# Attention's value projection computed as seven half-size products with the tokens stationary, its weight sums made in memory, and the input operands loaded ahead of it

## The chip, the cores and the metric

The kernel runs on one core of one Trainium2 chip. The metric is the device time of one execution in microseconds (us), as the median of several runs. Five engines run their own instruction streams and wait for each other by semaphores: PE (matrix multiplication, with its weight loads shown as PEld), DVE (vector), ACT (scalar, activations), POOL (GpSimd) and SP, which in this kernel only issues DMA transfers. Line numbers such as L256 are those of the kernel before.

## The reference, cut to what matters

One encoder layer over 512 tokens of width 2048, in float32:

```python
h = rms_norm(x, norm_mix_w[i])
proj = h @ w_in[i]
q_a, k_a, v_a, q_g, k_g, v_g, r_g, gate_lr = split_cols(proj, IN_SPLITS)
y_a = chunked_band_attention(q_a, k_a, v_a, att_rel_bias[i])     # 16 heads of 64
...
o_g = gated_linear_attention(q_g, k_g, v_g, log_a)               # 4 heads, state recurrence
o_g = rms_norm(o_g, gla_norm_w[i])
y_g = o_g * jax.nn.silu(r_g)
x = x + jnp.concatenate([y_a, y_g], axis=-1) @ w_out[i]
...                                                              # conv MLP, embedding, norm
```

The change concerns `v_a = h @ w_in[:, 2048:3072]` alone: 512 tokens by 2048 by 1024 columns.

## The kernel before, in words

**Number format.** Every float32 product is made of three matmuls on two-part operands. A weight page (128 x 1024, 512 KB) is loaded raw; ACT writes its high half (rounded), DVE its low half (raw less high); then high x high, high x low and low x high are accumulated. `wtile` (L118) does this for the first stages: it takes the next of three raw pages, three high pages and three low pages in rotation (the rings of L32), issues the load from SP, and queues the two halves on ACT and DVE. So the split of page n waits until PE is done with page n-3, and the load of page n+3 waits for the split of page n. It also pops one entry of the list `chores` (L116), if there is one.

**Stages.** First comes the normalised input `h1` (16 tiles of 128 x 2 x 512). Then, all from `h1`: the values of the linear attention (two calls of `vproj`, L234), then for its four heads a key and a query projection (`gla_proj`, L1150; `pk`, `pq`, 48 matmuls of 512 columns each) and the recurrence (`gla_core`, L1198: transposes `pkt`, scores `pat`, state updates `pu`, outputs `po`, a norm that goes through the sums `msw` and the root `rg`). Attention's values (`values_a`, L1076) are two more calls of `vproj`: the 128-token slices of `h1` are stationary, 512 weight columns move, 192 matmuls each, on 16 weight pages. `values_a(0)` stands before the last recurrence, `values_a(1)` after it.

After them the rest of the layer runs as Strassen-Winograd products: a 2 x 2 block product by seven half-size products P1, P2, P6, P5, P7, P3, P4 (L29) with the input operands R11, R21, N2, N1, T3, R22, T4 and the weight blocks or sums L11, L12, S2, S1, S3, S4, L22. The seven operands of the stage "in" (`front`) are made from the input early, by `input_pair`, and stored in memory as `h1d`; `Stage.load` (L342) brings each back in two tiles g = 0, 1 (512 KB each), and `Stage.split` (L348) makes its halves on ACT and DVE. Before the change six of these tiles (R11, R21, N2) are loaded after the linear attention's buffers are gone and split inside `values_a(1)` (`operand_step`); the other eight are loaded after it, when `h1` is free (`operands_left`), N1 is split there and T3, R22, T4 in the first steps of the stage.

**Sums in memory.** For some units the weight sums S1 to S4 are made by DMA: `sum_begin` copies one block to a scratch page in memory, and `sum_add`, issued by POOL, accumulates the other onto it. `chores` holds 18 such steps, for the first units of "wo" and "up", popped one at each `wtile` of the four heads.

**Order.** The Tile layer places the instructions of the early stages itself. Where the wrappers `vec`, `act`, `ten` (L55) are switched on, instructions stay in the order in which they are written; before the change that holds from the step loop on. On each engine the built order is fixed, and an instruction that waits holds up all behind it. The step loop takes a list `agenda` by step number.

Of the kernel before, what the change touches and what calls it, by code (L numbers as in the profile page):

```python
# [8 lines left out]
F32 = mybir.dt.float32  # L9
# [21 lines left out]
            "PP": ("L11", None, None)}  # L31
PLAIN = ("P1", "P2", "P6", "P5", "P7", "P3", "P4")  # L32
# [9 lines left out]
def encoder_block(ctx: ExitStack, tc: tile.TileContext, A, out):  # L42
# [27 lines left out]
    vec, act, ten = InOrder(nc.vector), InOrder(nc.scalar), InOrder(nc.tensor)  # L70

# [44 lines left out]
    chores = []  # L116

    def wtile(src, name, parts=1, between=None):  # L118
# [4 lines left out]
        for i in range(parts):  # L123
            if i and between is not None:
                between()
            c = slice(i * w, (i + 1) * w)
            nc.sync.dma_start(raw[:, c], src[:, c])
            nc.scalar.activation(hi[:, c], raw[:, c], AF.Copy)
            nc.vector.tensor_tensor(lo[:, c], raw[:, c], hi[:, c].bitcast(F32), ALU.subtract)
        if chores:  # L130
            chores.pop(0)()
# [102 lines left out]
    def vproj(src, c, evict, first=False, between=None, then=None):  # L234
        ps = [psum_mm(f"v{c}_{t}") for t in range(TT)]
        for kp in range(KD // 2):
            xs = []
# [65 lines left out]
    X_TAGS = [(op, g) for op in ("R11", "R21", "N2", "N1", "T3", "R22", "T4") for g in range(2)]  # L303

    def xtile(op, g, name, dt=F32R):
        pool = xa[0] if X_TAGS.index((op, g)) < 6 else xb[0]
        return pool.tile([P, 2, 1024], dt, tag=f"{op}{g}", name=name)
# [647 lines left out]

    for i, f in enumerate(sum_chores(summed[4:])):
        agenda[base[stages[4].units[2]] + 5 * i].append((0, f))
# [116 lines left out]
    vstage = {}  # L1074

    def values_a(c, between=None, then=None):  # L1076
        def place(t):
            vstage[c, t] = xslot(4 * c + t, "va")
            return vstage[c, t]

        vproj(A["w_v_a"], c, place, between=between, then=then)
        for t in range(TT):
            (nc.scalar if c else nc.sync).dma_start(vad[4 * c:4 * c + 4, :, t].rearrange("b p v -> p b v"),
                              vstage[c, t].rearrange("p (b v) -> p b v", b=4))
# [3 lines left out]
    with ExitStack() as mix:  # L1088
        vp = mix.enter_context(tc.tile_pool(name="v", bufs=1, side="right"))

        with ExitStack() as gctx:
# [21 lines left out]
            for c in range(2):  # L1113
                vproj(A["w_v_g"], c, lambda t: V[:, t, c * T:(c + 1) * T], c == 0, input_pair if c else None)

# [34 lines left out]
            def gla_proj(hd):  # L1150
# [39 lines left out]
                nc.vector.tensor_tensor(dd, kf, dd, ALU.mult)  # L1190
                pq = psum_mm("pq")
                proj(pq, [A["w_blk"][16 + hd, i] for i in range(2)], h1, f"wqg{hd}")
                qf = gt("qf", "kf")
                nc.vector.scalar_tensor_tensor(qf, pq, float(P) ** -0.5, rb, ALU.mult, ALU.mult)
                nc.vector.tensor_tensor(eb, qf, eb, ALU.mult)
                return eb, en, dd, dec2

            def gla_core(hd, eb, en, dd, dec2):  # L1198
# [3 lines left out]
                nc.vector.tensor_tensor(by_chunk(kd2), by_chunk(dd), each(dec2[:, 0:NCH]), ALU.mult)  # L1202
                eb2 = gt("eb2", "eb2")
                nc.vector.tensor_tensor(by_chunk(eb2), by_chunk(eb), each(dec2[:, NCH:2 * NCH]), ALU.mult)
                pkt = psum_aux("pkt")
                for t in range(TT):
                    sl = slice(t * P, (t + 1) * P)
                    nc.tensor.transpose(pkt[:, sl], kd2[:, sl], ident)
                kT = gt("kT", "kT")
                nc.scalar.activation(kT, pkt, AF.Copy)  # L1210
                pat = psum_aux("pat")
                for t in range(TT):
                    sl = slice(t * P, (t + 1) * P)
                    nc.tensor.matmul(pat[:, sl], en[:, sl], eb[:, sl], start=True, stop=True)
                for t in range(TT):
                    e0, o0 = t * P, t * P + CHUNK
                    nc.tensor.matmul(pat[0:CHUNK, o0:o0 + CHUNK], dd[:, e0:e0 + CHUNK], eb[:, o0:o0 + CHUNK],
                                     start=True, stop=True)
                at = attn_t[hd % 2]
                nc.vector.copy_predicated(at.rearrange("p (t j) -> p t j", j=P),  # L1220
                                          causal[:, None, :].broadcast_to([P, TT, P]),
                                          pat.rearrange("p (t j) -> p t j", j=P))

                S = [None] * TT
                for t in range(TT - 1):
                    pu = psum_aux("pu")[:, 0:256]
                    nc.tensor.matmul(pu, kT[:, t * P:(t + 1) * P], V[:, t, hd * 256:(hd + 1) * 256], start=True, stop=True)
                    S[t + 1] = gt(f"S{t + 1}", f"S{t + 1}", 1, 256)
                    if t == 0:
                        nc.vector.tensor_copy(S[1], pu)  # L1230
                    else:
                        d = 2 * NCH + t
                        nc.vector.scalar_tensor_tensor(S[t + 1], S[t], dec2[:, d:d + 1], pu, ALU.mult, ALU.add)

                o = []
                s2 = gt("s2", "s2")
                for vb in range(2):
                    po = psum_aux("po")
                    for t in range(TT):
                        sl = slice(t * P, (t + 1) * P)  # L1240
                        c0 = hd * 256 + vb * P
                        nc.tensor.matmul(po[:, sl], V[:, t, c0:c0 + P], at[:, sl], start=True, stop=t == 0)
                        if t > 0:
                            nc.tensor.matmul(po[:, sl], S[t][:, vb * P:(vb + 1) * P], eb2[:, sl], start=False, stop=True)
                    ov = xslot(8 + 2 * hd + vb, f"o{hd}_{vb}")
                    nc.vector.tensor_copy(ov, po)
                    if vb == 0:
                        nc.scalar.activation(s2, ov, AF.Square)
                    else:
                        s3 = tp.tile([P, T], F32, tag="sq", name="s3")  # L1250
                        nc.scalar.activation(s3, ov, AF.Square)
                        nc.vector.tensor_tensor(s2, s2, s3, ALU.add)
# [3 lines left out]
                nc.scalar.activation(sh, s2, AF.Copy)  # L1256
                nc.vector.tensor_tensor(sl, s2, sh.bitcast(F32), ALU.subtract)
                rstd_wide(ones_r, (sh, sl), 256, rg, gt("nwa", "nwa"))
                for vb in range(2):
                    nc.vector.scalar_tensor_tensor(o[vb], o[vb], gnw[:, vb:vb + 1], rg, ALU.mult, ALU.mult)  # L1260
# [321 lines left out]
```

## Time and profile before

| | |
|---|---|
| three runs | 2261.85, 2261.94, 2263.08 us; median 2261.94 |
| span of the profiled execution, first to last instruction | 2260.4 us |
| PE busy | 2245.6 us (99%), 18008 matmuls |
| DVE busy | 1859.7 us (82%) |
| ACT busy | 1298.9 us (57%) |
| DMA moved | 565.02 MB, 250 GB/s in the mean |

The page gives the span of the profiled execution; its own device time is not printed beside it, so 2260.4 is compared with the runs, which lie 1.5 us above it. "Busy" is the sum of the shown durations. A matmul's duration runs from its start to its modelled end and overlaps the next one, so the rate is read from the starts. A row of the timeline has the start and duration in us, the engine, the line, the operation, output<-inputs, shape, how many are merged, and in brackets how long the engine was idle before it and who ended that. Rows with SPq are DMA issues, not transfers.

### The profile page before, as it was taken

To read this page: it belongs to the slowest core of one execution; us is meant where nothing else is said; L and a number is where in the kernel's file an instruction comes from. 1 tells how busy PE (TensorE), PEld (TensorE's weight loads), DVE (VectorE), ACT (ScalarE), POOL (GpSimd) and SP (SyncE) were. 2 spreads that over 40 slices of the span, in tenths; PEclk is the share of its full clock that TensorE was granted. 3 is DMA by queue.
4 is the path that set the end of the run, shared out by engine and by line. 5 is a ranking of instruction groups with operands and counts; after the bars stand their busy time and mean duration, and the time that the engine had idled before them with its cause. 6 is when DMAs were issued, how large, how long until landed. Compare 5 with 4: busy or idle time off the path is not lost.

```text
span 2260.4 us, 45099 instructions
## 1 busy us (share of the span) xinstructions
PE 2245.6 (99%) x18008; PEld 2178.9 (96%) x18008; DVE 1859.7 (82%) x2562; ACT 1298.9 (57%) x1913; POOL 169.7 (8%) x209
## 2 busy tenths in 40 slices
PE   9999999999999999999999999999999999999997
PEld 8888889999999999999999999999999999999997
DVE  7567368998788888999888888888898797898987
ACT  6354367776665665555555555555564554666765
POOL 0010000000000001111111110000000100000000
PEclk9999999999999999999999999999999999999998
DMA  6994496666988979999999987877866967879896
GB/s 217 286 251 140 168 302 171 181 185 183 334 295 252 329 238 261 296 283 291 282 269 288 264 231 209 218 215 200 247 244 228 302 222 225 327 247 331 285 292 207
DMA packets 208882, 565.02 MB, mean 250 GB/s; under 512 B 22464, under 2 KB 73920, under 8 KB 208672
## 3 DMA queue, kind: packets, MB, share of 16 engines
q1 hardware_dynamic: 177536, 459.60, 57.3%
q0 software_dynamic: 27648, 99.10, 24.0%
q10 hardware_dynamic: 3488, 3.44, 0.4%
q8 instruction: 141, 2.31, 0.4%
q14 instruction: 69, 0.57, 0.1%
HBM read 483.41 MB, written 124.78 MB: 269 GB/s over the span
## 4 chain that ended last, share of the span: by engine, by line
PE 93%; DVE 3%; DMA 1%; ACT 1%; issue 1%; DVEq 0%; SPq 0%; POOL 0%; ACTq 0%; POOLq 0%
PE accA L64 44%; PE accC L64 22%; PE accB L64 11%; PE v L256 3%; PE v L258 3%; PE v L257 3%; PE pp L64 1%; PE psc L64 1%; PE ptr L64 1%; PE py L64 1%; DMA on<-ond 1%; DVE wl L64 1%; PE pq L137 1%; PE pq L136 0%; PE pq L135 0%
## 5 line engine op out<-in xcount | busy, mean ns | idle before, releaser
L64 DVE TENSOR_TENSOR wl<-s,wh 128x1024 fp32r<-128x1024 f32 (+1 forms) x365 | 438.1, 1201 | 67.2 <-ACT wh L64 66.3
L64 ACT ACTIVATE wh<-l 128x1024 fp32r<-128x1024 f32 (+1 forms) x308 | 319.0, 1037 | 184.4 <-PE accC L64 116.8
L64 DVE TENSOR_TENSOR wl<-l,wh 128x1024 fp32r<-128x1024 f32 (+1 forms) x308 | 367.8, 1194 | 57.4 <-ACT wh L64 57.1
L64 ACT ACTIVATE wh<-s 128x1024 fp32r<-128x1024 f32 (+1 forms) x365 | 378.1, 1036 | 28.2 <-DVE s L64 15.5
L64 ACT ACTIVATE u<-accA 128x256 f32<-128x256 f32 x290 | 109.6, 378 | 364.8 <-PE accA L64 364.7
L64 DVE TENSOR_TENSOR s<-s,l 128x1024 f32<-128x1024 f32 (+1 forms) x168 | 201.5, 1200 | 5.6 <-DMA s<-in_w_blk 5.2
L64 PE MATMUL accA<-up_T,wh 128*128 128x256 f32 x1408 | 178.8, 279 | 0.0
L64 PEld LDWEIGHTS accA<-up_T,wh 128*128 128x128 f32 x1408 | 170.3, 188 | 0.0
L64 DVE SCALAR_TENSOR_TENSOR cv<-u,cw,cv 128x511 f32<-128x511 f32 (+1 forms) x176 | 131.6, 748 | 3.1
L419 POOL DMA_DIRECT2D s<-in_w_up x84 | 74.2, 883 | 737.1 <-DMA s<-in_w_up 332.4
L256 PE MATMUL v<-wv_h,h 128*128 128x512 f32 x256 | 100.3, 392 | 0.0
L258 PE MATMUL v<-wv_h,h 128*128 128x512 f32 x256 | 100.1, 391 | 0.0
L257 PE MATMUL v<-wv_l,h 128*128 128x512 f32 x256 | 99.6, 389 | 0.0
L64 PE MATMUL accA<-up_T,wl 128*128 128x256 f32 x704 | 96.6, 279 | 0.0
L64 PE MATMUL accA<-dn_T,wh 128*128 128x256 f32 x704 | 89.9, 279 | 0.0
L64 PE MATMUL accA<-up_R,wh 128*128 128x256 f32 x704 | 89.8, 280 | 0.0
L64 PE MATMUL accB<-up_R,wh 128*128 128x256 f32 x704 | 89.4, 279 | 0.0
L64 PE MATMUL accC<-up_N,wh 128*128 128x256 f32 x704 | 89.4, 279 | 0.0
L64 PE MATMUL accC<-up_R,wh 128*128 128x256 f32 x704 | 89.4, 279 | 0.0
L64 PE MATMUL accA<-up_N,wh 128*128 128x256 f32 x704 | 89.4, 279 | 0.0
L64 PEld LDWEIGHTS accA<-up_T,wl 128*128 128x128 f32 x704 | 88.1, 188 | 0.0
L64 DVE TENSOR_TENSOR u<-u,accC 128x256 f32<-128x256 f32 x98 | 41.0, 418 | 57.2 <-PE accC L64 56.1
(410 smaller groups left out, 5131.6 us busy)
## 6 DMA issues: line engine op xcount, KB each, us to landing
l<-in_w_up SPq DMA_DIRECT2D x132, 512.0 KB, 6.5
s<-in_w_up SPq DMA_DIRECT2D x84, 512.0 KB, 6.0
s<-in_w_up POOLq DMA_DIRECT2D x84, 512.0 KB, 7.2
l<-in_w_dn SPq DMA_DIRECT2D x56, 448.0 KB, 5.0
l<-in_w_blk SPq DMA_DIRECT2D x36, 512.0 KB, 4.8
l<-in_w_out SPq DMA_DIRECT2D x28, 512.0 KB, 5.0
l<-in_w_dn SPq DMA_DIRECT2D x28, 512.0 KB, 4.9
s<-in_w_blk SPq DMA_DIRECT2D x24, 512.0 KB, 4.7
```

What stands on the lines that cost most here:

```text
L64: ins = f(*args, **kw)
L137: nc.tensor.matmul(po, wlo, act[:, 0, :], start=False, stop=stop)
L256: nc.tensor.matmul(ps[t], h1[kt][:, 0, sl], wh, start=kt == 0, stop=False)
L257: nc.tensor.matmul(ps[t], h1[kt][:, 0, sl], wl, start=False, stop=False)
L258: nc.tensor.matmul(ps[t], h1[kt][:, 1, sl], wh, start=False, stop=kt == KD - 1)
L419: nc.gpsimd.dma_start(t, src("L22" if name == "S1" else "L11"), accum_op=ALU.add)
```

## The change

**The product.** `values_a` goes. Attention's values become seven products of half size, from the operand tiles of `front` instead of `h1`: per product 4 weight pages, per page two blocks of 128 rows, two token slices, three matmuls of 512 columns, so 12 matmuls per page, 28 pages, 336 matmuls in all against 384. Four pages of each of P1, P2, P4 come from the weights; P6, P5, P7, P3 read pages S2, S1, S3, S4 that 16 DMA copies and 16 accumulating DMAs have made in memory (18 `value_chores`, four of them popped in the first `vproj`, the others in the four heads, none in the second `vproj`). The seven results are gathered by ACT and DVE into four quarters and stored to `vad`.

```diff
+    def values_begin():
+        v = dict(ps=[psum_mm(f"va{i}") for i in range(4)], pages=[(p, j) for p in PLAIN for j in range(4)], tiles={}, have=set())
+        for n in range(2):
+            value_fetch(v, n)
+        return v
+    def value_fetch(v, n):
+        if n < len(v["pages"]):
+            prod, j = v["pages"][n]
+            v["tiles"][n] = wtile(value_page(PRODUCTS[prod][0], j), f"wva_{prod}{j}")
+    def values_product(v, prod, between=None):
+        _, op, b = PRODUCTS[prod]
+        acc2 = v["ps"][0:2] if b == "A" else v["ps"][2:4]
+        fresh = prod in ("P1", "P2", "P5")
+        for j in range(4):
+            n = 4 * PLAIN.index(prod) + j
+            value_fetch(v, n + 2)
+            if between is not None:
+                between(j)
+            hi, lo = v["tiles"].pop(n)
+            for i in range(2):
+                k = 2 * j + i
+                x = front.x[op, k // 4]
+                wh, wl = hi[:, i * T:(i + 1) * T], lo[:, i * T:(i + 1) * T]
+                for t in range(2):
...
+                    ten.matmul(acc2[t], x[:, 0, sl], wh, start=first, stop=False, **kw)
+                    ten.matmul(acc2[t], x[:, 0, sl], wl, start=False, stop=False, **kw)
+                    ten.matmul(acc2[t], x[:, 1, sl], wh, start=False, stop=last, **kw)
+    def values_collect(v, prod):
...
+            if quarter not in v["have"]:
+                act.activation(dst, acc2[i], AF.Copy, scale=float(sign))
+            else:
+                vec.tensor_tensor(dst, dst, acc2[i], ALU.add if sign > 0 else ALU.subtract)
+            if quarter in v["have"] or quarter == "C21":
+                (nc.scalar if c else nc.sync).dma_start(vad[4 * c:4 * c + 4, :, 2 * h + i].rearrange("b p v -> p b v"),
...
```

**Its place.** It needs the operands, so `h1`'s buffers are given up and the first eight operand tiles (R11, R21, N2, N1) are loaded into them right after the last head's query projection; the other six follow after P2. What is left of the last two recurrences (`gla_core` is now a generator) is written between the pages of P1 and P2, with the wrappers on, so in written order. The splits of all operands stand between the pages, those of T3, R22, T4 no longer in the step loop.

```diff
-            for hd in range(1, 4):
+            for hd in range(1, 3):
                 nxt = gla_proj(hd)
-                gla_core(hd - 1, *st)
+                for _ in gla_core(hd - 1, *st):
+                    pass
                 st = nxt
-            values_a(0)
-            gla_core(3, *st)
+            cores = [gla_core(2, *st)]
...
+            nxt = gla_proj(3, middle)
+            cores.append(gla_core(3, *nxt))
+            hctx.close()
...
+            for op, g in X_TAGS[:8]:
+                front.load(op, g)
+            in_order(True)
+            va = values_begin()
+            for g in range(2):
+                front.split("R11", g)
+            step(0)
+            nxt[-1]()
+            def beside_first(j):
+                if j:
+                    step(0)
+                if j > 1:
+                    front.split("R21", j - 2)
+                    step(1)
+            def beside_second(j):
+                step(1)
+                if j % 2:
+                    front.split("N2", j // 2)
+            values_product(va, "P1", beside_first)
+            values_collect(va, "P1")
+            values_product(va, "P2", beside_second)
+            values_collect(va, "P2")
...
+    for op, g in X_TAGS[8:]:
         front.load(op, g)
...
+    values_product(va, "P6", lambda j: front.split("N1", j // 2) if j % 2 else None)
+    values_collect(va, "P6")
+    values_product(va, "P5", lambda j: front.split("T3", j // 2) if j % 2 else None)
...
```

**The other sums.** The 18 chores of "wo" and "up" move from the heads into the step loop:

```diff
+    for i, f in enumerate(sum_chores(summed[:4])):
+        agenda[2 + 5 * i + 3 * max(i - 10, 0)].append((0, f))
...
-    for n, op in enumerate(("T3", "R22", "T4")):
-        for g in range(2):
-            agenda[2 * n + g + (n > 0)].append((3, lambda op=op, g=g: front.split(op, g)))
...
-            chores.extend(sum_chores(summed[:4]))
```

**The built order around it** (P10 is page 0 of P1, and so on; "high" and "low" are the halves of a page or an operand tile; "a > b" means that b stands behind a):

```
PE    last pq: 20 matmuls > pkt, pat of head 2 > 28 matmuls > pu > P10 > po > P11 > msw > P12 >
      pkt, pat of head 3 > P13 > pu > P20 > po > P21 > msw > P22 > P23 > P60 ... P43 (12 matmuls each) > pp
ACT   high P10 > kT > high P11 > high R11.0 > high R11.1 > high P12 > high P13 > two squares > s2h >
      high P20 > Ln > Exp (rg) > high R21.0 > high P21 > high R21.1 > kT ...
      second norm: s2h > high N2.0 > high P60 > Ln > Exp > high P61
DVE   kf > low P10 > en, dd, kd2, eb2 > mask > low P11 > low R11.0 > low R11.1 > three states S > two for eb >
      low P12 > low P13 > two copies of po > sum > s2l > low P20 > four for rg > low R21.0 > kd2 (head 3) ...
      second norm: s2l > low N2.0 > low P60 > four for rg > low P61 > two scalings > low N2.1 >
      P2's two gathers > low P62 > low P63
SP    loads P10, P11, P12, P13, P20 > R11.0 .. N1.1 (eight) > P21, P22, P23, P60 .. P63, P50 >
      two stores of head 3 > two stores of a quarter > T3.0 .. T4.1 (six), p > P51, P52, P53 ...
```

More of the change, by code (lines that the diff above doesn't have):

```diff
@@ L31 @@
             "PP": ("L11", None, None)}
+PRODUCT_OPERANDS = ("R11", "R21", "N2", "N1", "T3", "R22", "T4")
 PLAIN = ("P1", "P2", "P6", "P5", "P7", "P3", "P4")
@@ L236, in vproj @@
         for kp in range(KD // 2):
+            if first and kp == 4:
+                chores.extend(value_chores())
             xs = []
@@ L1072, in norm_root @@
         norm["w"] = rstd_begin(norm["ms"])
[L1074 to L1084, printed above, removed]
+    value_sums = {}
```

154 lines of the change are left out of this document (98 added, 56 removed).

## The prediction

> **What bounds the kernel now.** I read the page first, then the waits of PE, then the timeline around the changed stretch (195 to 308 us), engine by engine.
>
> ```profile
> span 2260.4 us, 45099 instructions
> ...
> PE 2245.6 (99%) x18008; PEld 2178.9 (96%) x18008; DVE 1859.7 (82%) x2562; ACT 1298.9 (57%) x1913; POOL 169.7 (8%) x209
> ...
> PE   9999999999999999999999999999999999999997
> ...
> DMA  6994496666988979999999987877866967879896
> ```
>
> ```profile
> PE pb L64 <- DVE dg L64: 1.7, 1, 1.7
> ...
> PE accA L64 <- DVE wl L64: 0.8, 1, 0.8
> ```
>
> PE is the bound from end to end, and its longest wait anywhere is 1.7 us, in the tail. So a matmul less is time less, but only while PE stays fed; there is no old stall to remove, and every new one is paid in full. DMA is emptiest in the fourth and fifth slices (4 tenths, 170 to 283 us): there the change puts its page loads.
>
> **The gain: 48 matmuls.** The rate is read from the first and the last start of one `pq`:
>
> ```profile
> 114.20 0.39 PE L135 MATMUL pq<-h,wqg_h 128*128 128x512 f32 x1
> ...
> 124.86 0.40 PE L137 MATMUL pq<-h,wqg_l 128*128 128x512 f32 x1
> ```
>
> 47 steps in 10.66 us are 0.227 us each. 384 - 336 = 48 matmuls fewer, the shape and format unchanged: **-10.9 us**. A page lasts 12 x 0.227 = 2.72 us where it lasted 5.44.
>
> **The price: what PE waits for.** The new stretch runs in written order, so I follow it by hand. Zero is the start of the last `pq`. The rows of the old recurrence give its parts:
>
> ```profile
> 206.35 0.60 PE L1208 MATMUL pkt<-ident,kd 128*128 128x128 f32 x4
> ...
> 208.38 1.56 PE L1227 MATMUL pu<-Vg,kT 128*128 128x256 f32 x6
> ...
> 210.48 0.61 PE L1242 MATMUL po<-attnT,Vg 128*128 128x128 f32 x4
> ...
> 213.38 0.39 PE L1244 MATMUL po<-eb,S 128*128 128x128 f32 x2
> ```
>
> `pkt` with `pat` takes 208.38 - 206.35 = 2.0, `pu` about 1.3 (1.56 less the overlap at its end), `po` 213.6 - 210.5 = 3.1. Since 206.35 ends a `pq` of 10.9, the old zero is 195.45; the old stretch ends where `pp` begins:
>
> ```profile
> 308.09 11.32 PE pp L64 x48
> ```
>
> Old length: 112.6. The new work by its parts is 10.9 + 2 x (2.0 + 1.3 + 3.1 + 0.5 for `msw`) + 336 x 0.227 = 100.9 (112.6 - 10.9 = 101.7 agrees within 1). DVE, ACT and the loads:
>
> ```profile
> 207.16 0.68 DVE L1202 TENSOR_TENSOR kd<-dd,dec 128x512 f32<-128x512 f32 x1
> 207.76 0.69 DVE L1195 TENSOR_TENSOR eb<-qf,eb 128x512 f32<-128x512 f32 x1
> ...
> 210.12 0.41 DVE L1230 COPY S<-pu 128x256 f32<-128x256 f32 x1
> 210.63 1.06 DVE L1233 SCALAR_TENSOR_TENSOR S<-S,dec,pu 128x256 f32<-128x256 f32 x2
> ...
> 213.80 0.69 DVE L1246 COPY pair_u<-po 128x512 f32<-128x512 f32 x1 [0.65 <-PE po L1244]
> ...
> 216.58 0.69 DVE L1257 TENSOR_TENSOR s2l<-s,s2h 128x512 fp32r<-128x512 f32 x1 [0.70 <-ACT s2h L1256]
> ...
> 285.95 2.35 DVE L64 TENSOR_TENSOR in_R<-in_R 128x1024 fp32r<-128x1024 f32 x2
> ```
>
> ```profile
> 216.57 1.28 ACT L64 ACT_TABLE_LOAD   x1
> 217.87 0.69 ACT L64 ACTIVATE rg<-msw,epst 128x512 f32<-128x512 f32 x1
> 218.57 1.28 ACT L64 ACT_TABLE_LOAD   x1
> 219.87 0.63 ACT L64 ACTIVATE rg<-rg 128x512 f32<-128x512 f32 x1
> ...
> 281.30 1.06 ACT L64 ACTIVATE in_R<-in_R 128x1024 fp32r<-128x1024 f32 x1 [4.75 <-DMA in_R<-h_R]
> 282.58 1.06 ACT L64 ACTIVATE in_R<-in_R 128x1024 fp32r<-128x1024 f32 x1 [0.22 <-DMA in_R<-h_R]
> ```
>
> ```profile
> 275.71 2.16 SPq L346 DMA_DIRECT2D in_R<-h_R x4
> 277.92 1.31 SPq L346 DMA_DIRECT2D in_N<-h_N x2
> 279.27 0.61 SPq L931 DMA_DIRECT2D pT<-in_p  x1
> 279.98 0.41 SPq L127 DMA_DIRECT2D wv_r<-in_w_v_a  x1
> ```
>
> So 0.6 per DVE operation of 512 columns (207.16 to 207.76), 1.6 for the three states, 1.2 for a low half, 1.1 for a high half; an operand tile is usable by ACT 281.30 - 275.71 = 5.6 after the first issue, the next 1.3 later.
>
> 1. *R11 is late.* SP issues R11 behind page P20, which needs the raw page of P11 split, which needs the high page of `pq`'s first half: 20 matmuls (4.5) + `pkt`, `pat` (2.0) + 4 matmuls = 7.5; high and low P11 make it 9.8, R11 issues at 10.3, lands at 15.9, its high half is done at 17.0, its low at 18.2. PE is free at 10.9 + 2.0 + 1.3 = 14.2. P10 begins with high x high but its third matmul needs the low half: it ends at 18.2 + 10 x 0.227 = 20.5 in place of 16.9: **+3.6**. Behind the waiting DVE and ACT instructions stand the states of head 2 and P12, P13.
> 2. *The first norm.* `po` runs to 23.6, P11 to 26.3, then `msw` needs `s2l`. DVE does low R11.1, the states, two for `eb`, low P12 and low P13 (whose high half needs P10's page back, 20.5 + 1.1) first: 24.6; then two copies, and from the second copy to the end of `s2l` the old rows need 217.27 - 213.80 = 3.5: 28.7. **+2.3**.
> 3. *The scores of head 3 stand behind the root.* P12 runs 29.1 to 31.8, then `pkt` needs `kd2`, which DVE has behind the four for `rg` and low R21.0. ACT: `s2h` at 28.1, high P20 1.0, table 1.3, Ln 0.7, table 1.3, Exp 0.6: 33.0; DVE: 3 x 0.6 + 1.2 + 0.7: 36.7. **+4.9**. In the old order `kd2` was done at 207.8 and the last `pkt` came 50 us later, behind `values_a(0)`:
>
> ```profile
> L1208 PE MATMUL pkt<-ident,kd x16: 270/272/273, 147.1 to 257.5; 128*128 128x128 f32 x16
> ```
>
> 4. *The second norm.* PE goes on: `pkt`, `pat` to 38.8, P13 41.5, `pu` 42.8, P20 45.5, `po` 48.6, P21 51.3, `msw` when `s2l` is there, 52.1 to 52.4 (**+0.6**), P22 and P23 to 57.8. No matmul needs this root, but DVE has it ahead of page halves: ACT `s2h` 51.4, two high halves 2.1, tables, Ln, Exp 3.9: 57.4; DVE 3 x 0.6, low P61 1.2, two scalings and two gathers 2.5, low N2.1 1.2, low P62 1.2: 65.3. PE reaches P62 at 57.8 + 5.4 = 63.2: **+2.1**.
> 5. *P51 behind seven loads.* SP may issue T3 to T4 and `p` only after P2's gathers (64.1) and two stores (1.2, as two load issues), at 65.3; P51 stands behind them, 7 x 0.55 later, 69.3. The old trace has the same pattern, a page (issued at 279.98) behind seven such loads:
>
> ```profile
> wv_r<-in_w_v_a SPq DMA_DIRECT2D x2, 512.0 KB, 7.2
> ```
>
> That lands P51 at 76.5, halves at 78.8; PE is done with P50 at 73.4 (57.8, four pages of P6 and P50, the 2.1): **+5.2**. After it a page's raw buffer comes free some 8 us before it is needed, and a lone page lands in 3.5:
>
> ```profile
> wv_r<-in_w_v_a SPq DMA_DIRECT2D x16, 512.0 KB, 3.5
> ```
>
> so the remaining 14 pages flow.
>
> Sum: 3.6 + 2.3 + 4.9 + 0.6 + 2.1 + 5.2 = 18.7. Work and waits are 100.9 + 18.7 = 119.6 in place of 112.6: **+7.0 us**. Its bounds: with no wait at all -10.9, with each half as long again +16.
>
> *At no cost.* The value gathers (ACT, DVE, 0.7 each) lie beside the next product, which writes another pair of banks; without that cover they cost 1.3 per product. ACT's two stores of C22 wait for DVE's gathers after P7 and hold high P32 up: 1.3 + 1.1 for the issues + 1.1 + 1.2 = 4.7 after P7, where P32 is wanted two pages (5.4) after it: nil, with 0.7 to spare. The 16 + 16 value sums replace chores of the same size in the heads, where DMA was full (9 tenths in the second and third slices) and PE never waited. The splits of T3, R22, T4 leave the first steps, where PE did not wait either: no gain. The first unit's sum pages load only when raw pages come free, P43's some 6 us before the end, but `pp` (11.3) stands ahead of them; without it the delay would be on the path.
>
> *The moved sums of "wo" and "up".* In the step loop they meet these:
>
> ```profile
> 400.00:420.00 20.00, 20.00 (x178) 19.52 (x177) 18.10 (x40) 13.18 (x25) 1.73 (x2) 1.00 0.73 197
> ...
> 600.00:620.00 20.00, 20.00 (x159) 19.37 (x159) 16.75 (x22) 14.19 (x21) 0.00 (x0) 1.00 1.01 386
> ```
>
> (the last two columns: DMA share, GB/s). Most fall where a quarter of the DMA time is free, a pair in some 19 us: nil. The last few fall about 600 to 690, where DMA is full; POOL also queues the units' own accumulations behind each. Below: 0; above: the four transfers at about 2 us of traffic each, 8 us. I take 0.5, since PE rode out a full queue there without a wait.
>
> Total: 2260.4 + 7.0 + 0.5 = 2267.9 of span; the median of the runs, 2261.94, lies 1.5 above the span: **2269 us**.
>
> **The rivals.**
>
> *The loads are in time (20%).* If R11 lands before `pq` ends and P51 beside P6, waits 1 and 5 go and wait 2 shrinks to 0.8: 0.8 + 4.9 + 0.6 + 2.1 = 8.4 against 10.9, 2259.5 us. For it: the empty DMA slices. Against it: what is late is the issue, by SP's order, not the rate.
>
> *The count rules (10%).* If waits 2 to 4 are covered too: 2262 - 10.9 = 2251 us. It needs `kd2` to be done before P12 ends, against the DVE order.
>
> *The sums collide (12%).* The moved sums delay the loads of "wo" by the upper 8: 2276 us. It decides from the step where POOL's accumulation lands after its unit needs it.
>
> *The clock falls (13%).* In the old tail PE runs dry:
>
> ```profile
> 2245.00:2250.00 5.00, 2.46 (x23) 2.13 (x21) 4.12 (x14) 4.08 (x10) 0.00 (x0) 0.90 0.66 228
> 2250.00:2255.00 5.00, 1.19 (x2) 0.48 (x2) 3.60 (x6) 2.25 (x5) 0.00 (x0) 0.50 0.84 293
> ```
>
> The granted clock (third column from the end) is 0.90, then 0.50, within a few us of idling. Waits 1, 3 and 5 idle PE for 3.6, 4.9 and 5.2 us. If each were followed by as long a time at half rate, half of 13.7 us would be lost: 2269 + 6.9 = 2276 us. The Trainium skill (TensorE: Matmul & The Clock Gate, Part 1: The HAM clock gate) states that an idle window of about 3.4 us halves the clock and about 3.4 us of sustained work restores it; by that, an estimate, three falls cost 3 x 1.7 = 5 us. The fall agrees with the rows above; the return no row here shows.
>
> **How the numbers follow.** The forecast has 45%, at 2269, itself between 2265 and 2274. The range takes in the loads in time and both dear rivals and leaves out the count: 2255 to 2278. A change of 0.2% (4.5 us) is what a measurement tells from none. Slower by more: most of the forecast's 45% and the two dear rivals, 64%; within: the loads in time and the forecast's low end, 23%; faster: the count and the edge of the loads in time, 13%.
>
> **What would show it.** PE waits on L64 (the wrapper) between 205 and 320 us: `va` for in_R, `msw` for `s2l`, `pkt` for `kd`, `va` for a low page twice, the last with a DMA behind it; `pp` starting about 315 instead of 308.09; and 2.72 us a page between. Wrong it would be if PE has no waits there (then `pp` starts near 297), or if `pp` is on time and the loss appears after 560.

## The result, and the profile after

| | before | after |
|---|---|---|
| median of the runs, us | 2262.51 (2261.85 to 2264.63) | 2303.16 (2298.81 to 2304.33) |
| span of the profiled execution | 2260.4 | 2300.8 |
| first `pp`, in the chain | 308.09 | 334.39 |
| second `pp`, in the chain | 616.90 | 653.31 |

After over before is 1.0178, with a 95% interval from 1.0163 to 1.0192: slower by 40.4 us of span, where +7.5 was forecast. The page of the changed kernel:

```profile
span 2300.8 us, 45116 instructions
...
PE 2252.0 (98%) x17960; PEld 2180.4 (95%) x17960; DVE 1878.6 (82%) x2580; ACT 1312.1 (57%) x1925; POOL 183.8 (8%) x225
...
PE   9998799999989999999999999999999999999997
...
DMA  7985578888898898999999987777786876968896
```

There are 48 matmuls fewer, and yet more busy time: a matmul at a lower clock is a longer one. PE's row has dents in the fourth and fifth slice (173 to 288 us) and in the twelfth (633 to 690 us). The waits of PE up to 720 us (line of the waiting instruction, who ended the wait; us in total, times, longest):

```profile
PE pkt L65 <- DVE kd L65: 9.4, 2, 4.8
PE va L65 <- ACT wva_P_h L65: 7.2, 1, 7.2
PE accC L65 <- DVE wl L65: 6.7, 2, 3.7
PE accA L65 <- ACT wh L65: 3.3, 1, 3.3
PE va L65 <- DVE wva_P_l L65: 1.8, 2, 1.3
...
PE va L65 <- ACT in_R L65: 1.3, 1, 1.3
...
PE v L263 <- ACT wv_h L65: 1.0, 1, 1.0
```

Where the 40.4 us lie follows from three marks that both programs have: the start of the last `pq` group (195.08 before, 199.12 after), the first `pp`, the second `pp`. The last two stand in the chain (the work that ended last, followed back from the end), the kernel before first:

```profile
616.90 11.20 PE pp L64 x48
```

```profile
334.39 10.73 PE pp L65 x46
...
653.31 11.21 PE pp L65 x48
...
665.50 14.01 DMA wo_N<-mix_N
```

- **Up to the last `pq`: +4.0.** The second values projection of the linear attention is longer: PE waits twice in it, 1.8 us in all, and then works 3.4 us at half rate.
- **From there to the first `pp`: +22.3** (135.3 us against 113.0). Here lies the stretch that the prediction follows.
- **From the first to the second `pp`: +10.1** (318.92 against 308.81), in the last units of the stage "in".
- **Behind it: +4.0** in the stage "wo", whose operand wo_N takes 14 us to come in; after that both programs run in step.

In the stretch PE's waits add up to 21.4 us in ten places. The clock fell at four of them. These are the four pieces at half rate: after the times come the length and PE's busy time, and the third column from the end is the granted clock.

```profile
208.95:212.37 3.42, 3.42 (x20) 2.98 (x19) 0.50 (x1) 0.60 (x1) 0.00 (x0) 0.50 0.41 149
222.61:226.02 3.41, 3.41 (x8) 2.71 (x9) 2.19 (x4) 1.93 (x2) 0.00 (x0) 0.50 1.02 412
239.67:246.50 6.83, 4.45 (x22) 4.01 (x23) 6.83 (x9) 1.85 (x3) 0.00 (x0) 0.50 0.25 49
284.05:294.29 10.24, 4.95 (x11) 3.61 (x12) 4.92 (x5) 5.82 (x7) 0.00 (x0) 0.50 0.55 206
```

They stand at `pkt` of head 2 (its wait ends at 208.45), R11 (221.28), `pkt` of head 3 (242.05) and P51 (288.88). PE is busy again there and still runs at half rate, for 3.4 to 5 us. What is left over prices it: 22.3 = -10.9 (matmuls gone) + 2.2 (a slower step, below) + 21.4 (waits) + 9.6 (slow clock). The four pieces hold 16.2 us of PE's work at half rate, which is a loss of 8.1; the other 1.5 of the 9.6 stay open.

The slower step: the prediction took 0.227 us for the 336 new matmuls. Two rows of the new ones lie 39 matmuls apart:

```profile
317.90 0.63 PE L65 MATMUL va<-wva_P_h,in_R 128*128 128x512 f32 x2
...
327.00 0.40 PE L65 MATMUL va<-wva_P_h,in_T 128*128 128x512 f32 x1
```

9.10 / 39 = 0.2333 us, the step of `pp` in both kernels (11.20 / 48); 336 x 0.0066 = 2.2 us, so the gain is 8.7 and not 10.9.

### The profile page after: what moved, and what is told of

It is laid out like the page before. It is cut to its first block, busy times and chain, and to the rows that moved or that the text cites. A ratio compares the mean times of both kernels' runs of the same rounds, so it can differ in the third digit from the quotient of the medians.

```text
span 2300.8 us, 45116 instructions
## 1 busy us (share of the span) xinstructions
PE 2252.0 (98%) x17960; PEld 2180.4 (95%) x17960; DVE 1878.6 (82%) x2580; ACT 1312.1 (57%) x1925; POOL 183.8 (8%) x225
## 4 chain that ended last, share of the span: by engine, by line
PE 85%; DMA 5%; DVE 5%; ACT 2%; issue 1%; SPq 0%; DVEq 0%; ACTq 0%
PE accA L65 42%; PE accC L65 21%; PE accB L65 10%; PE va L65 2%; DVE wl L65 1%; PE pp L65 1%; PE psc L65 1%; DMA on<-ond 1%; DMA wv_r<-in_w_v_g 1%; PE ptr L65 1%; PE py L65 1%; PE v L264 1%; PE v L263 1%; PE v L265 1%; DMA wo_N<-mix_N 1%
## 5 line engine op out<-in xcount | busy, mean ns | idle before, releaser
L65 ACT ACTIVATE u<-accC 128x256 f32<-128x256 f32 x94 | 36.0, 383 | 89.5 <-PE accC L65 88.8
L65 PEld LDWEIGHTS accA<-dn_T,wh 128*128 128x128 f32 x704 | 85.7, 188 | 0.0
L65 PEld LDWEIGHTS accA<-up_R,wh 128*128 128x128 f32 x704 | 85.2, 188 | 0.5 <-issue 0.5
```

The source lines that it names most:

```text
L65: ins = f(*args, **kw)
```

## The experiments

All by medians beside runs of the kernel before on the same chip (2262.1 to 2264.6); "pp to pp" is from the first to the second in the chain.

| run | median, us (range) | ratio, 95% interval | first pp | pp to pp |
|---|---|---|---|---|
| after | 2303.16 (2298.81 to 2304.33) | 1.0178 (1.0163 to 1.0192) | 334.39 | 318.92 |
| moved sums alone | 2279.02 (2277.61 to 2281.83) | 1.0072 (1.0057 to 1.0087) | 308.49 | 320.24 |
| idle time filled | 2298.73 (2298.50 to 2301.89) | 1.0161 (1.0145 to 1.0176) | 330.37 | 317.81 |
| kd2 earlier | 2290.35 (2285.37 to 2293.09) | 1.0118 (1.0103 to 1.0133) | 321.93 | 319.29 |
| loads one by one | 2291.49 (2289.43 to 2298.43) | 1.0132 (1.0111 to 1.0152) | 324.32 | 318.52 |
| value sums later | 2298.11 (2296.07 to 2304.43) | 1.0158 (1.0143 to 1.0174) | 329.51 | 318.59 |
| moved sums closer | 2294.12 (2290.58 to 2300.99) | 1.0135 (1.0119 to 1.0151) | 332.97 | 314.80 |
| all four edits | 2272.42 (2270.72 to 2276.99) | 1.0040 (1.0028 to 1.0053) | 313.49 | 312.10 |
| six edits | 2274.59 (2272.21 to 2285.41) | 1.0054 (1.0039 to 1.0068) | 319.50 | 317.29 |
| output sums beside the values | 2285.57 (2282.25 to 2287.79) | 1.0096 (1.0083 to 1.0109) | 329.15 | 308.88 |
| old values, order held | 2278.51 (2277.70 to 2280.54) | 1.0067 (1.0054 to 1.0080) | 323.85 | 308.22 |
| up sums in "wo" | 2275.81 (2274.64 to 2278.68) | 1.0062 (1.0049 to 1.0075) | 315.11 | 307.66 |
| R11 placed | 2282.97 (2280.63 to 2286.38) | 1.0092 (1.0078 to 1.0105) | 320.76 | not read |

A caution on the first `pp`: in the profiled execution of the changed kernel the clock fell behind the two short waits at 91 us. In four runs with the same order up to there (idle time filled, kd2 earlier, loads one by one, moved sums closer) PE waits there too, 1.5 to 2.3 us in all, but the clock stays full and that projection ends 1.2 to 1.7 us sooner. That much of their gain in the first `pp` is not their edit's.

### The moved sums alone

The kernel before, with only the 18 steps of the output and up sums moved as the change moves them:

```diff
+    for i, f in enumerate(sum_chores(summed[:4])):
+        agenda[2 + 5 * i + 3 * max(i - 10, 0)].append((0, f))
...
-            chores.extend(sum_chores(summed[:4]))
```

> The kernel before, with only the 18 sum steps of wo and up moved from the heads into the step loop, as the change does. Theory 'sums collide': the changed kernel lost 14 us behind the value stretch (pp at the end of stage in comes 10.1 later still, wo another 4), where DMA is full from 592 to 696 us, and all of it comes from these steps: 2273 to 2277 us, with PE waits of 3 us each on a low half (wl) of the last units of stage in and on a high half (wh) in wo. Rival 'the late start': the loss comes from stage in starting with its pages loaded late behind the new value product; then the moved steps alone cost nothing: 2261 to 2264 us.

Measured +16.3 us, even a little more than expected, with the values stage untouched (first `pp` 308.49 against 308.09) and all of the loss behind it. It is the changed kernel's own loss there: the same two waits on low weight halves in the last units of "in", the same wait in "wo". The kernel after shows where:

```profile
616.64 1.65 PE L65 MATMUL accC<-in_N,wl 128*128 128x256 f32 x6 [3.65 <-DVE wl L65]
```

```profile
600.00:620.00 20.00, 16.34 (x127) 16.14 (x126) 14.00 (x20) 9.35 (x13) 2.57 (x3) 0.88 1.01 284
620.00:640.00 20.00, 19.07 (x154) 18.87 (x153) 9.03 (x11) 7.59 (x10) 0.00 (x0) 0.95 1.05 347
```

The DMA share (last but one column) is 1.0 here in the kernel before too, and PE had no wait then; the clock is 0.88 beside the wait. What is late is no weight page. The chain leads from this low half (`wl`) over DVE to loads of the linear attention's outputs (`on`); DVE waits for the second of them ahead of the half that PE needs, and for another ahead of the half that ends PE's next wait, at 642.1:

```profile
592.28 13.29 DMA on<-ond
605.63 6.92 DMA on<-ond
```

```profile
612.64 1.23 DVE L65 TENSOR_TENSOR u<-u,on 128x1024 f32<-128x1024 f32 x1 [3.03 <-DMA on<-ond]
...
638.09 1.23 DVE L65 TENSOR_TENSOR u<-u,on 128x1024 f32<-128x1024 f32 x1 [6.75 <-DMA on<-ond]
```

In the kernel before the longest of these four loads took 9.5 us, and DVE waited 1.7 us for them in all; it waits 11.7 us in the changed kernel and 12.2 with the moved sums alone.

### Idle time filled

The changed kernel with matmuls of no use ahead of two long waits, 18 before head 3's `pkt` and 30 before P51, so that PE waits less idly and ends no sooner:

```diff
+    def fill(op, n):
+        x = front.x[op, 0]
+        po = psum_aux("fill")
+        for _ in range(n):
+            ten.matmul(po, x[:, 0, 0:P], x[:, 0, 0:T], start=True, stop=True)
```

> The changed kernel with idle matmuls whose results are not used: 18 of 512 columns ahead of the transposes of head 3, 30 ahead of page P51, so that PE works while it waits there. The waits themselves stay. Theory 'the clock': of the stretch's 135.3 us, 100.9 are work and 21.4 shown waits; the other 13 are matmuls at half clock after the waits, 2.3 of them after these transposes and about 4 after P51. Filled, these two go: 2303 - 6.5, 2296 to 2298 us, and the granted clock stays at 1.00 in both places. Rival 'no clock': the 13 us are something else, and filling brings nothing or costs: 2302 to 2306 us.

The first `pp` comes 4.0 us sooner, though PE does 48 matmuls more. Of this 1.2 us lie ahead of the edit (the last `pq` begins at 197.89 and not at 199.12), so the stretch itself is 2.8 us shorter. The granted clock behind both places is full, where it was 0.84 and 0.74:

```profile
240.00:260.00 20.00, 18.81 (x105) 15.51 (x105) 14.56 (x19) 9.46 (x12) 0.00 (x0) 1.00 0.35 106
...
280.00:300.00 20.00, 18.68 (x80) 14.53 (x79) 10.86 (x10) 12.18 (x15) 0.00 (x0) 1.00 0.68 236
```

So idle time, and not the new instructions, lowers the clock. By the pieces at half rate above (4.45 and 4.95 us of work) these two falls had cost 4.7 us; the median fell by 4.4, a little less than expected. (The profiled run was the highest of the four, 2301.89.)

### kd2 earlier

The recurrence's `kd2` and `eb2` written one step sooner for heads 2 and 3, so that DVE has them before the norm's operations:

```diff
             cores = [gla_core(2, *st)]
             step = lambda n: next(cores[n], None)
+            step(0)
...
-                for n in range(2):
-                    step(0)
+                step(0)
...
+                if j == 1:
+                    step(1)
                 if j > 1:
                     front.split("R21", j - 2)
+                if j == 3:
                     step(1)
```

> The changed kernel with the two scaled keys (kd2, and eb2) of heads 2 and 3 written earlier: head 2 ahead of the last key projection, head 3 right behind s2l instead of behind the root. Theory 'order of DVE, with the clock': both waits of pkt go (4.63 and 4.79) and the half clock after them (1.8 and 2.3): 13.5 us less, 2288 to 2291 us. Order without the clock: 9.4 less, 2293 to 2295 us. Rival 'the wait moves on': DVE and the loads are late anyway and the time comes back at the next page or at P51: 2298 to 2303 us.

As expected: both waits on `kd` are gone and the first `pp` is 12.5 us sooner: 9.4 of waits gone, 1.2 more for R11, and the rest mostly clock (part of it ahead of the edit). PE now comes to R11 on time and waits for it in full, in two pieces:

```profile
214.99 0.50 PE L65 MATMUL va<-wva_P_h,in_R 128*128 128x512 f32 x1 [2.48 <-ACT in_R L65]
...
216.25 0.73 PE L65 MATMUL va<-wva_P_h,in_R 128*128 128x512 f32 x2 [0.53 <-DVE in_R L65]
```

That is 3.0 us, where the prediction has +3.6; in the changed kernel the late `pkt` had hidden a part of it.

### Loads one by one

The six late operand tiles and p no longer all ahead of P51:

```diff
-    for op, g in X_TAGS[8:]:
-        front.load(op, g)
...
+    def beside_p5(j):
+        front.load(*late_loads.pop(0))
+        if j > 1:
+            front.split("T3", j - 2)
```

> The changed kernel with the six loads of T3, R22, T4 and that of p issued one by one between the later pages instead of all ahead of P51. Theory 'SP's order': the wait for P51 (7.25 and 0.46) goes with the half clock after it (about 4): 11 to 12 us less, 2290 to 2293 us. Rival 'the rate of DMA': the same bytes are late whichever comes first; P51 is in time but an operand tile or a later page is not: 2300 to 2304 us.

As expected: the wait of 7.25 us for P51's high half is gone (0.31 and 0.76 are left on low halves), the first `pp` is 10.1 us sooner, 1.5 of them ahead of the edit. SP's order was the cause.

### Value sums later

```diff
-            if first and kp == 4:
-                chores.extend(value_chores())
...
+            chores.extend(value_chores())
             st = gla_proj(0)
```

> The changed kernel with the 18 steps of the value sums begun at the head stage's first projection, not in the middle of the first values projection. First theory: the 4.0 us that the second values projection takes longer (19.36 us instead of 15.35, with PE waits of 1.03 and 0.76 on wv pages that land late and a clock of 0.61 behind them) come from the value sums' accumulates among the stores of that stretch, so the second values projection is back at about 15.4 us and the median is about 2299 (2297 to 2301). Rival, the 4 us come from something else in the changed program: no change, 2302 to 2304. Second rival, the sums cost the head stage as much as they cost here: the second projection is back at 15.4, but the last pq starts no earlier than 199, and the median stays at 2302 to 2304.

The first theory holds. In the changed kernel two accumulates go out on POOL at 77.16, among the operand stores, and the next page of the second projection takes 10.3 us to land (chain); PE waits for its halves. They are written in the first projection, but in the built order they stand on POOL behind the clearing of a buffer (`up_r`), which waited 54 us:

```profile
77.16 1.66 POOL L1099 DMA_DIRECT2D va_S<-in_w_v_a  x2
```

```profile
79.67 10.26 DMA wv_r<-in_w_v_g
```

```profile
91.13 0.50 PE L263 MATMUL v<-wv_h,h 128*128 128x512 f32 x1 [1.03 <-ACT wv_h L65]
```

In the experiment no PE time is lost there (20.00 of 20 busy, clock 1.00), the first `pp` is 4.9 sooner and the median 5.0 lower:

```profile
80.00:100.00 20.00, 20.00 (x89) 16.48 (x88) 6.01 (x6) 7.97 (x11) 1.82 (x2) 1.00 0.88 292
```

### Moved sums closer

```diff
-        agenda[2 + 5 * i + 3 * max(i - 10, 0)].append((0, f))
+        agenda[2 + 4 * i].append((0, f))
```

> The changed kernel with the 18 moved steps of the output and up sums four step-loop steps apart throughout (the last at step 70; in the changed kernel they reach further, five and then eight apart). First theory: their 14 to 16 us come of the stretch from 592 us on, where the DMA share is already 1.0 and where an accumulate more makes the pages of wl and wh late; sums that are done before it cost little there, the waits on wl at 616.6 and 642.1 and on wh at 681.8 shrink or go, and the median is 2287 to 2292. Rival, the bytes cost the same wherever in the step loop they stand, since the loop's first stage is as full: the waits come earlier by name but the sum is the same, 2300 to 2306.

9 us came back of the 14 to 16, less than expected, and 1.4 of them in the first `pp`, ahead of the edit. The last sum goes out at 595.6, still inside the full slices, and one wait on wl is left; the wait in "wo" is gone:

```profile
PE accC L65 <- DVE wl L65: 3.9, 1, 3.9
```

### All four edits

The four edits above together.

> The changed kernel with four edits at once: kd2 and eb2 of heads 2 and 3 written a step earlier, the late operand loads and p one by one behind P51's first pages, the value sums begun at the head stage's first projection, the moved sums four steps apart. First theory, the four terms are independent (13, 12, 4 and 11 to 16 us): 2303 less 40 to 45, that is 2258 to 2263, level with the kernel before (2262.5). Rival, the stretch keeps part of its slow clock behind the waits that are left (R11's 1.3 to 3 us, the second norm's): 2264 to 2272. Rival, the early sums and the value sums collide with the operands' loads: above 2275.

2272.4: three quarters of the loss gone, and some 9 us short of level. The first rival is nearest, but what is left is one wait that had been small. Two of the value sums' accumulates, pushed back by the later start, stand on POOL behind an instruction that waits for the head stage's end, and then run among R11's loads:

```profile
198.61 1.66 POOL L1097 DMA_DIRECT2D va_S<-va_S  x2 [0.36 <-issue]
```

```profile
PE va L65 <- ACT in_R L65: 6.0, 1, 6.0
```

The clock behind it was about half for 4 us more. The other rest is one wait of 2.8 on wl.

### Six edits, and the output sums beside the values

The first takes two further edits: the value sums' first two copies at once, so that nothing is left over for POOL at the end, and the moved sums three steps apart. The second puts the output sums beside the values' pages and leaves only the up sums in the step loop:

```diff
+            ready = value_chores()
+            ready.pop(0)()
+            ready.pop(0)()
+            chores.extend(ready)
...
-    for i, f in enumerate(sum_chores(summed[:4])):
+    for i, f in enumerate(sum_chores(summed[2:4])):
         agenda[2 + 4 * i].append((0, f))
...
+            chores.extend(sum_chores(summed[:2]))
```

> All four edits again, with two more: the value sums' first two copies go out before the head stage's first projection, so that their last two accumulates no longer stand on POOL behind the head stage's end (in the run with all four edits they went out at 198.6 us, among R11's loads, and PE waited 6.0 us for R11); and the moved sums stand three steps apart, so that the last is out before the DMA-full stretch. Theory: R11's wait falls from 6.0 to 1 to 3 us and the slow clock behind it (2.4 us) goes with it, the 2.8 us wait on wl and its 1.9 us of slow clock go: 2272.4 less 5 to 9, that is 2263 to 2267. Rival, R11 is late by SP's order and not by the two accumulates: 2270 to 2273. Rival, sums three steps apart make pages late inside the head attention units: 2272 to 2280.

> As the run with the six edits, but the output sums (8 of the 16) are made beside the values' pages from P12 on, where the DMA share was 0.45 to 1.0, and only the up sums are left in the step loop, four steps apart, done by some 450 us. Theory: the step loop's first stage costs nothing more against the kernel before, and the values' pages have room: 2259 to 2265, level with or under the kernel before (2262.5). Rival, the pages and late operands of P5 to P4 land late (they have the 1.0 slice): more waits on low pages there, 2265 to 2275.

Both missed what was hoped for. The wait for R11 fell to 4.3 and 4.4, but with the copies taken at once the first head's `pz` waited 5.9 and 3.8 us for DVE's `lr` (the chain leads to a weight page, `wqg_r`, which took 16.5 us to land in the first), so the head stage ended later. The first run has the range of its last rival. Its profile, of one of its two dear executions out of six, shows the wait on wl down to 0.2 us, but a new one of 4.5 us at 462.6, inside an attention unit, with a sum page in its chain that took 12.4 us to land. The second run shows one thing clearly. With eight accumulates in the step loop, done at 465 us, the first stage is as short as before:

```profile
329.15 11.20 PE pp L65 x48
...
638.03 11.30 PE pp L65 x48
```

308.88 against 308.81: there the sums are free, as the prediction said. Beside the values they are not: the 126.5 us from `pq` to `pp` are 10 more than with the four edits, and the waits on page halves have grown from 2.8 to 10.5 us.

### The old values, order held

```diff
-                    nc.tensor.matmul(ps[t], h1[kt][:, 0, sl], wh, start=kt == 0, stop=False)
+                    tc.keep_in_program_order(nc.tensor.matmul(ps[t], h1[kt][:, 0, sl], wh, start=kt == 0, stop=False))
```

(and so for the other two matmuls of `vproj`, in the kernel before).

> The kernel before with the four values projections' matmuls held in program order, nothing else. It asks why a matmul of the new values products starts 0.233 us after the one ahead of it where one of the old starts 0.227 us after it (336 of them: 2.3 us that the prediction left out). Theory A, the held order costs it (the pp products, held too, step at 0.233 in both kernels): the 768 matmuls of the four projections step at 0.233 and the median rises by about 5 us, to 2267. Theory B, it is the operands or the banks: steps of 0.227, no change, 2262 to 2263.

Theory B for the step: 52 matmuls between two rows take 11.79 us, 0.2267 each.

```profile
80.00 0.39 PE L256 MATMUL v<-wv_h,h 128*128 128x512 f32 x1
...
91.79 0.39 PE L257 MATMUL v<-wv_l,h 128*128 128x512 f32 x1
```

What makes the new matmuls step at 0.2333 stays open. The median rose all the same, by 15.5 us, for a reason that neither theory had: matmuls that can't be moved no longer fill the recurrence's waits. PE stood 2.83 us before `msw` twice, and what follows shows the price of one such wait in the clock:

```profile
222.23 0.50 PE L64 MATMUL msw<-s2h,ones_r 128*128 128x512 f32 x1 [2.83 <-ACT s2h L1256]
...
224.31 0.63 PE L256 MATMUL v<-wv_h,h 128*128 128x512 f32 x1
224.74 0.63 PE L257 MATMUL v<-wv_l,h 128*128 128x512 f32 x1
```

Steps of 0.43 in place of 0.227 from 223.9 to 226.9, after an idle time of 2.83 us. The 5.8 us that this run has lost by its last `pq` lie at one place too: PE waits 3.66 us for `dg` ahead of `pb`, up to 49.48, and works at half rate from 49.51 to 52.92.

### The up sums in "wo", and R11 placed

```diff
-    for i, f in enumerate(sum_chores(summed[:4])):
+    for i, f in enumerate(sum_chores(summed[:2])):
         agenda[2 + 4 * i].append((0, f))
+    for i, f in enumerate(sum_chores(summed[2:4])):
+        agenda[base[wo.units[2]] + 4 * i].append((0, f))
```

and in the second also two steps of the value sums taken ahead of the last head's projections, and R21, N2, N1 loaded a page later each.

> The run with all four edits, but of the moved sums only the output's 8 stand in the step loop's first stage (four steps apart, done by about 450 us); the up sums' 8 stand in the output stage, where the DMA share of the kernel before is 0.66 to 0.85 for 100 us. Theory, the moved sums cost time only where they reach the full DMA slices from 560 us on (the run with 8 sums four steps apart had the first stage as short as the kernel before: 308.89 us from the first to the second pp, against 308.81): the 2.8 us wait on wl and its slow clock go, 312.1 becomes 309, nothing is lost in the output stage, and the median is 2268 to 2270. Rival, the accumulates delay the output stage's own additions or weight pages: 2272 or more.

> The same, with two edits for R11: two of the value sums' steps are taken together before the last head's projections, so that their last accumulates go out before POOL waits for the head stage's end, and only R11's two loads are issued at that end, R21, N2 and N1 one product page later each. Theory, R11 is late because its loads share the DMA engines with two accumulates and two to six other operand loads: PE's wait for it falls from 6.0 to 1 to 3 us, the half-rate stretch behind it (2.4 us) goes, and the median is 2261 to 2265, level with the kernel before (2263). Rival, it is late by SP's order and its own transfer: a wait of 4 to 6 us, 2266 to 2270. Rival, the later loads make R21 or N2 late: 2270 or more.

The first ends at its rival's 2272 or more. The stage "in" is 1.2 us shorter than in the kernel before, but 7.7 us are lost behind it (the second `pp` is 5.9 later than before, the span 13.6 longer): the last up sums run into the full slices of 740 to 800 us.

```profile
766.22 1.21 PE L65 MATMUL accA<-wo_N,wl 128*128 128x256 f32 x8 [1.57 <-DVE wl L65]
```

R11 placed went wrong: in the built order the two steps' copies left SP only at 200.4, so not two but four accumulates fell among R11's loads, and the wait is the longest of all:

```profile
206.96 2.50 POOL L1099 DMA_DIRECT2D va_S<-va_S  x3 [0.76 <-DMA va_S<-in_w_v_a]
```

```profile
PE va L65 <- ACT in_R L65: 11.4, 1, 11.4
```

With none (kd2 earlier, six edits, output sums beside the values), two, two and four accumulates there the wait was 3.0 to 4.4, 6.0, 6.2 and 11.4 us, and from R11's first issue to its first high half it took 4.7 to 6.5, 7.9, 7.9 and 13.6 us. It is no clean series, as the loads differ too, but it goes one way. No version beats the kernel before; the nearest, with four edits, is 0.4% behind it.

## Why the prediction was wrong in size

The sign and the likeliest mechanism held: slower, because PE waits in the new stretch. The size failed, +7.5 against +40.4, of which 18.1 lie outside that stretch, by these steps.

| step of the prediction | forecast | measured | by |
|---|---|---|---|
| the gain, 48 x 0.227 | -10.9 | -8.7 | the step of 0.2333 |
| 1, R11 | +3.6 | 1.8; 3.0 with `pkt` on time | waits, kd2 earlier |
| 2, first norm | +2.3 | 0.9 | waits |
| 3, `pkt` of head 3 behind the root | +4.9 | 4.8 | waits, kd2 earlier |
| `pkt` of head 2 | 0 | 4.6 | waits, kd2 earlier |
| 4, second norm, P62 | +2.7 | 1.5 | waits |
| 5, P51 behind seven loads | +5.2 | 7.7 | waits, loads one by one |
| slow clock in the stretch | 0 (rival, 6.9) | 9.6 left over, 8.1 of it in the pieces at half rate | windows; idle time filled |
| value sums | 0 | 4.0; 2.3 to 2.9 where the clock did not fall | value sums later |
| moved sums | 0.5 (rival, 8) | 14.1; 16.3 alone | moved sums alone |

**Waits 3 and 5** were right in cause and, within 2.5 us, in size; each went away with the edit that takes its cause. Wait 1 has the cause that the prediction gives, as far as the rows show (with kd2 earlier SP is at the pages up to 209.1 and issues R11 at 209.16), but no edit took it away; that it measured half is due to the late `pkt`. Waits 2 and 4 were smaller. That these five waits come to 16.7 where 18.7 was forecast is in part luck, since their errors offset each other.

**The first step that failed is in wait 1: "20 matmuls (4.5) + `pkt`, `pat` (2.0)", with no wait between.** Head 2's `kd2` stands on DVE behind `kf`, `en`, `dd` of head 3, and DVE comes to that `kf` late, after its work for the norm of the head before. The kernel before shows when; the row was not looked up:

```profile
201.09 0.68 DVE L1188 TENSOR_TENSOR kf<-pk,rb 128x512 f32<-128x512 f32 x1
```

That is 6.0 us after the last `pq` begins (195.08), later than the 4.5 of 20 matmuls, and `kd2` is still to come. In the old order all 48 matmuls of `pq` stood ahead of that `pkt`; the new one puts it after 20. In the kernel after, where `pq` begins at 199.12, it is the same with `kf`, and 3.8 us from its start to `pkt`:

```profile
204.68 0.68 DVE L1258 TENSOR_TENSOR kf<-pk,rb 128x512 f32<-128x512 f32 x1
...
207.62 0.68 DVE L65 TENSOR_TENSOR kd<-dd,dec 128x512 f32<-128x512 f32 x1
```

```profile
208.45 0.63 PE L65 MATMUL pkt<-ident,kd 128*128 128x128 f32 x4 [4.63 <-DVE kd L65]
```

**The second is the sum itself, which has the waits and not the clock.** The prediction sets the clock beside the sum as a rival of 13%, though its own sum has three waits of 3.6 to 5.2 us and its own rows show the fall. It was no alternative but a consequence: 9.6 us in the stretch, against 21.4 of waits. The rule of the Trainium skill (TensorE: Matmul & The Clock Gate, Part 1: The HAM clock gate) is half the clock after an idle window of about 3.4 us and the full one after as long at work. The return agrees: 3.4 to 5 us of work at half rate, then the full clock. The fall agrees for long waits: in the kept traces, up to 850 us, all 35 waits of PE of 3.4 us and more have half rate behind them. But so have eight of the eleven of 2.2 to 3.3 us, such as those of 2.83 us with the order held. The 1.7 us a fall that the prediction works out from that rule was near (1.7 to 2.5 here); there were four falls, one at the wait that it did not have, and not three.

**The third and dearest is the price of the moved sums, "I take 0.5, since PE rode out a full queue there without a wait".** That PE has no wait beside a full queue says that nothing is late yet, not that there is room. The bound from above, 8 us, in the sum and in the rival, was the four transfers' own time. What they delay cost more: the loads of `on`, for which DVE waits ahead of weight halves, the 14 us of wo_N, and a slow clock behind the two waits of the stage "in". The other half of the step was right: the sums are free at 350 to 465 us.

**The fourth is the value sums "at no cost", as "chores of the same size".** They are, but four of the 18 steps no longer stand in the heads; they stand in the first values projection, beside the operand stores, and a page of the next one took 10.3 us to land. The text on the change says where they are popped; the step of the prediction looked at the heads alone.

## What to carry to other kernels

Where a kernel is at 98% of one engine, a new wait of 2 us or more is mostly paid twice, in idle time and then in a slow clock: put the clock into the sum with the waits. The second part hardly grows with the wait: 1.9 us behind one of 6.0 (all four edits), 3.0 behind one of 11.4 (R11 placed). When work is moved up in an engine's order, look up when each of its inputs was ready in the old trace, also the ones that nobody waited for. A queue that is full and harmless has no room: extra accumulates belong where the DMA share is below one until they are done, and a step beside a full slice is priced by what it delays, not by its own bytes.

## What the runs showed of the hardware that was not expected

- Two groups of matmuls of one shape and format, 128x512 with the clock granted in full, step at 0.2267 (`v`, `pq`) and at 0.2333 us (`va`, `pp`). Holding the order does not make the difference (0.2267 with it); what does stays open.
- The clock fell after less idle time than the three long waits have: steps of 0.43 us after one of 2.83 us. The two waits of 1.03 and 0.76 us at 91 us brought 3.4 us at half rate in one execution, and two such waits at the same place none in four others.
- The pieces at half rate last 3.4 us or a whole multiple: 3.4, 3.4, 6.8 and 10.2 in the stretch, 13.7 around R11's wait of 11.4 us.
- Two accumulates cost a plain load beside them much time: a 512 KB page took 10.3 us to land, where the same page took 4.7 in the kernel before and 4.4 with the value sums later. Other pages of that projection took up to 7.2 without them.
